# Rotating 96 images by 90 degrees: all slabs turned in pairs, every row 16 KB, the first pair stored between the loads

## The chip, the cores and the metric

The kernel runs on one core of a Trainium2 chip. The metric is device time in microseconds (us) of that core. Beside the three timed runs there is one profiled execution; its span goes from its first to its last instruction. A DMA (a transfer between HBM, the chip's main memory, and SBUF, the core's working memory of 128 partitions) is issued by an instruction on a queue, here the queue of SyncE (SP), and is carried out by 16 DMA engines as packets. VectorE is DVE in the profile, ScalarE is ACT.

## The reference

```python
x = np.random.randn(32, 3, 256, 256).astype(np.float32)
out = np.rot90(x, k=-1, axes=(-2, -1))       # out[b, c, i, j] = x[b, c, 255 - j, i]
```

Nothing is calculated: 96 images of 256 x 256 float32 values (256 KB each, 25.17 MB in all) are read, each is rotated clockwise, and 25.17 MB are written.

## The kernel before, in words

**Slabs.** The 24,576 image rows are cut into 12 slabs of 2 MB (8 images). A slab fills one tile of 128 partitions by 4096 floats, its *unit* (`units`, lines 71 to 79), and all twelve units together hold the whole input at once, 192 KB in each partition. A partition holds either 8 image rows in one piece twice over ("short" rows of 8 KB, line 63), or 16 image rows in one piece ("long" rows of 16 KB, line 66). A long slab is moved by two DMAs of 1 MB, each to every second partition (`i::I`).

**The turn.** VectorE's transpose turns 32x32 blocks: it moves data within groups of 32 partitions. Rotating a whole image therefore needs a change of layout between load and store, which the access patterns of `turn` (lines 102 to 118) make: read with the image rows spread one way, write with both orders reversed. A slab that is turned by itself has short rows on one side and long rows on the other. Slabs 0, 1 and 2 (`long_st`) are loaded short and stored long; slabs 3 to 7 are loaded long and stored short. Slabs 8 to 11 (`paired`) are turned two at a time, (8, 9) and (10, 11): one turn over both units, in four instructions, with long rows on both sides. Each instruction of a turn handles 128 x 2048 floats, so there are 24 in all.

**Homes.** A turn doesn't write where it reads. `home` (line 100) puts slab n's result into slab n-1's unit, which is free once slab n-1 has been turned. (For the pairs, the results go one pair back: lines 110 and 111.) Slab 0 has nothing before it: its result goes into `turned0`, a tile in PSUM, the other on-chip memory, which a DMA doesn't read here. At the end ScalarE copies it into the last unit by two copies (line 146), and it is stored from there (line 148).

**Queues.** All DMAs are issued by SP, in program order: the loads of slabs 0, 1, 2, 3, 7, 4, 5, 6, 8 to 11 (line 86; the first half of the last slab in two pieces, rows of 14 KB and 2 KB, line 94), then the stores of 4, 3, 5, 6, 7, 1, 2 (line 136), then those of the pairs, then slab 0's. Lines 139 and 140 hold the first store back until the 14 KB piece has landed. The DMAs share eight completion semaphores in turn: DMA number k is issued only when DMA number k-8 has landed. VectorE turns slab after slab in order of number.

Of the kernel before, what the change touches and what calls it, by code (L numbers as in the profile page):

```python
# [1 line left out]

# [4 lines left out]

@with_exitstack
def kernel(
    ctx: ExitStack,
    tc: tile.TileContext,
    x: bass.AP,
    out: bass.AP,
):

    nc = tc.nc
    fp32 = mybir.dt.float32

    B, C, H, W = x.shape
    P = nc.NUM_PARTITIONS
    RL, RS = 16, 8  # L50
    I = 2
    Q = P * RS // H
    n_slabs = B * C // (Q * I)
    last = n_slabs - 1
    F = RS * W
    long_st = (0, 1, 2)
    both = (8, 10)
    paired = [n + a for n in both for a in range(2)]

    rows_in = x.rearrange("b c h w -> (b c h) w")  # L60
    rows_out = out.rearrange("b c h w -> (b c h) w")

    def short(rows):
        return rows.rearrange("(n i p r) w -> n p i (r w)", i=I, p=P, r=RS)

    def long(rows):
        return rows.rearrange("(n i m r) w -> n i m (r w)", i=I, m=P // I, r=RL)

    ld_short, ld_long, st_short, st_long = short(rows_in), long(rows_in), short(rows_out), long(rows_out)

    units = [None] * n_slabs
    adjacent = [(3, 7), (8, 9), (10, 11)]
    pairs = []
    for us in adjacent + [(u,) for u in range(n_slabs) if all(u not in us for us in adjacent)]:
        pool = ctx.enter_context(tc.tile_pool(name=f"unit{us[0]}", bufs=1))
        held = pool.tile([P, len(us), I * F], fp32, name=f"u{us[0]}")
        for j, u in enumerate(us):
            units[u] = held[:, j]
        pairs.append(held)
    psum = ctx.enter_context(tc.tile_pool(name="psum", bufs=1, space=bass.MemoryType.PSUM))  # L80
    turned0 = psum.tile([P, I * F], fp32, name="turned0")

    def fours(t):
        return t.rearrange("p (i f) -> p i f", i=I)

    for n in (0, 1, 2, 3, 7, 4, 5, 6, *range(8, n_slabs)):
        if n in (1, 2):
            nc.sync.dma_start(out=fours(units[n]), in_=ld_short[n])
            continue
        for i in range(I):  # L90
            if n in long_st:
                ld = nc.sync.dma_start(out=fours(units[n])[:, i], in_=ld_short[n][:, i])  # L92
            else:
                cuts = (0, 14 * W, RL * W) if (n, i) == (last, 0) else (0, RL * W)
                for f0, f1 in zip(cuts, cuts[1:]):
                    ld = nc.sync.dma_start(out=units[n][i::I, f0:f1], in_=ld_long[n, i][:, f0:f1])
                    if f1 == 14 * W:
                        mark = ld

    home = [turned0] + units[:last]  # L100

    def turn(n):
        if n in long_st:
            src = fours(units[n]).rearrange("p i (r g c) -> p c r g i", r=RS, c=RL)
            dst = home[n].rearrange("p (c k r) -> p c r k", c=RL, r=RS)[:, :, ::-1, ::-1]
            parts, step = 2, RL // 2
        elif n in paired:
            if n not in both:
                return
            src = pairs[both.index(n) + 1].rearrange("p a (r g c) -> p c r g a", r=RL, c=RL)  # L110
            dst = pairs[both.index(n)].rearrange("p i (c k r) -> p c r k i", c=RL, r=RL)[:, :, ::-1, ::-1, :]
            parts, step = 4, RL // 4
        else:
            src = units[n].rearrange("p (r g c) -> p c r g", r=RL, c=RS)
            dst = fours(home[n]).rearrange("p i (c k r) -> p c r k i", c=RS, r=RL)[:, :, ::-1, ::-1, :]
            parts, step = 2, RS // 2
        for h in range(parts):
            nc.vector.transpose(out=dst[:, h * step : (h + 1) * step], in_=src[:, h * step : (h + 1) * step])  # L118

    def store(n):  # L120
        if n in paired:
            first = n if n in both else n - 1
            if n == first:
                nc.sync.dma_start(out=st_long[n].transpose([1, 0, 2]), in_=pairs[both.index(n)][::I])
                return
            for i in range(I):
                nc.sync.dma_start(out=st_long[n, i], in_=pairs[both.index(first)][n - first :: I, i])
        elif n in long_st:
            for i in range(I):
                nc.sync.dma_start(out=st_long[n, i], in_=home[n][i::I])  # L130
        else:
            return nc.sync.dma_start(out=st_short[n], in_=fours(home[n]))

    for n in range(both[0]):
        turn(n)
    for n in (4, 3, 5, 6, 7, 1, 2):
        st = store(n)
        if n == 4:
            tc.add_manual_dep(st.ins, mark.ins.name, mybir.DependencyInfo(
                mybir.DependencyClass.Sync, mybir.DependencyReason.SCHED_ONLY), reason="stores after loads")  # L140
    for n in range(both[0], n_slabs):
        turn(n)
        store(n)

    for i in range(I):
        nc.scalar.copy(out=fours(units[last])[:, i], in_=fours(turned0)[:, i])  # L146
    home[0] = units[last]
    store(0)


# [1 line left out]
_INS = ['x']  # L152
_OUTS = [((32, 3, 256, 256), 'float32')]


# [23 lines left out]
```

## Time and profile before

| what | value |
|---|---|
| three timed runs | median 123.25 us (123.1, 123.25, 123.28) |
| profiled execution, span | 121.4 us |
| what lies around the span, by the median | 123.25 - 121.4 = 1.85 us |
| first DMA issued, first transpose, end of last transpose | 0.73, 8.25, 99.06 us |
| ScalarE: table load, two copies | 1.3 us at 62.3; 3.6 us from 99.1 |
| DMAs: loads, stores | 23 and 17 |
| HBM read, written | 25.17 MB, 25.17 MB |
| granted TensorE clock | 1.000 (TensorE does nothing) |

The profile gives no total for the profiled execution apart from its span; the median of the runs stands 1.85 us above it. The 17 stores are 7 of 2 MB and 10 of 1 MB. All DMAs go through one queue, so the 16 engines work through them in the order of issue. A "packet" in the profile is one contiguous row, and each DMA ends with 16 packets of 4 bytes, one for each engine, which count up its semaphore: 40 x 16 = 640 of them.

### The profile page before, as it was taken

The page shows a single profiled execution, that of the slowest core. Times are in us where ns is not written, and L with a number is a line of the kernel's source. Part 1 is how long each engine was busy: PE and PEld are TensorE (multiplying, and loading weights), DVE is VectorE, ACT ScalarE, POOL GpSimd, SP SyncE. Part 2 cuts the span into 40 slices and gives each one's busy share as a digit, 9 for nine tenths or more (in the row PEclk, how much of TensorE's full clock was granted, in tenths as well). Part 3 has the DMA queues.
Part 4 walks back from the last instruction along what each step waited for, and adds up shares of the span by engine and source line. Part 5 has one row for each costly group of instructions (what it writes and reads, how often), then busy time and mean ns, then how long its engine had stood idle before and what let it go on. Part 6 is the DMA issues. An engine that isn't in the chain of part 4 may idle for free.

```text
span 121.4 us, 134 instructions
## 1 busy us (share of the span) xinstructions
DVE 90.5 (75%) x24; ACT 4.9 (4%) x3; POOL 0.2 (0%) x4
## 2 busy tenths in 40 slices
DVE  0029999999999999999999999999999960000000
ACT  0000000000000000000040000000000038000000
POOL 0000000000000000000000000000000000000000
DMA  3999999999999999999999999999999999999994
GB/s 84 416 432 424 426 459 432 432 432 426 426 432 426 416 421 432 421 426 450 403 424 426 426 429 429 421 432 424 464 426 432 432 432 432 432 432 432 432 432 178
DMA packets 4800, 50.33 MB, mean 414 GB/s; under 512 B 640, under 2 KB 640, under 8 KB 704
## 3 DMA queue, kind: packets, MB, share of 16 engines
q1 hardware_dynamic: 4800, 50.33, 98.0%
HBM read 25.17 MB, written 25.17 MB: 414 GB/s over the span
## 4 chain that ended last, share of the span: by engine, by line
DVE 55%; issue 17%; DMA 6%; DVEq 3%; ACT 2%; ACTq 1%; SPq 0%
DVE u L118 50%; DVE turned L118 6%; DMA u<-in_x_dram 6%; DVEq L174 3%; ACT u L146 2%; ACTq L174 1%; SPq L92 0%; DVEq L118 0%
## 5 line engine op out<-in xcount | busy, mean ns | idle before, releaser
L118 DVE STREAM_TRANSPOSE u<-u 128x2048 f32<-128x2048 f32 x22 | 83.4, 3861 | 0.3
L118 DVE STREAM_TRANSPOSE turned<-u 128x2048 f32<-128x2048 f32 x2 | 7.1, 3584 | 8.3 <-DMA u<-in_x_dram 8.3
L146 ACT COPY u<-turned 128x2048 f32<-128x2048 f32 x2 | 3.6, 1869 | 35.6 <-DVE u L118 35.6
L146 ACT ACT_TABLE_LOAD x1 | 1.3, 1283 | 62.3 <-DMA u<-in_x_dram 62.3
L163 POOL MEMSET const-uint8-127<- 128x1 uint8 x1 | 0.1, 103 | 0.0
L163 POOL MEMSET const-bfloat16-1.0<- 128x1 bf16 x1 | 0.1, 101 | 0.0
L163 POOL MEMSET const-float32-0.0<- 128x1 f32 x1 | 0.1, 99 | 0.2 <-issue 0.2
L163 POOL MEMSET const-float32-1.0<- 128x1 f32 x1 | 0.1, 99 | 0.0
## 6 DMA issues: line engine op xcount, KB each, us to landing
u<-in_x_dram SPq DMA_DIRECT2D x19, 1024.0 KB, 19.6
out_dram<-u SPq DMA_DIRECT2D x7, 2048.0 KB, 16.3
out_dram<-u SPq DMA_DIRECT2D x10, 1024.0 KB, 18.3
u<-in_x_dram SPq DMA_DIRECT2D x2, 2048.0 KB, 13.7
u<-in_x_dram SPq DMA_DIRECT2D x1, 896.0 KB, 19.3
u<-in_x_dram SPq DMA_DIRECT2D x1, 128.0 KB, 17.2
```

Source lines behind the costliest of these rows:

```text
L118: nc.vector.transpose(out=dst[:, h * step : (h + 1) * step], in_=src[:, h * step : (h + 1) * step])
L146: nc.scalar.copy(out=fours(units[last])[:, i], in_=fours(turned0)[:, i])
L163: nc = _bacc.Bacc("TRN2", target_bir_lowering=False, num_devices=1)
L174: with _tile.TileContext(nc) as tc:
```

## The change

Slabs are replaced by six *pairs* of 4 MB (16 images). Pair n fills one unit of 128 partitions by 2 x 4096 floats; six units again hold the whole input. Every pair is turned as slabs 8 to 11 were: four transposes of 128 x 2048, long rows of 16 KB on both sides. A pair is loaded by four DMAs of 1 MB (64 rows of 16 KB to every second partition, of one half of the unit) and stored by two of 2 MB (128 rows of 16 KB, from every second partition).

The result of pair n goes into the unit of pair n-1, and that of pair 0 into the unit of pair 5, which is still empty: the pairs 0 to 3 are loaded, pair 0 is turned and stored, and then the pairs 4 and 5 are loaded, the latter into the unit that pair 0 is stored from. Stores of the pairs 1 to 5 follow. `move` chains all DMAs so that they are issued in this order; the edge orders them on the queue and waits for nothing. The PSUM tile, the ScalarE copies, the short rows, the 14 KB and 2 KB pieces and the hold of lines 139 and 140 are gone. There are 24 loads and 12 stores.

```diff
-    RL, RS = 16, 8
-    I = 2
...
-    long_st = (0, 1, 2)
-    both = (8, 10)
-    paired = [n + a for n in both for a in range(2)]
+    R, I, A = 16, 2, 2
+    M = P // I
+    n_pairs = B * C // (A * I * P * R // (I * H))
+    last = n_pairs - 1
...
+    def rows(t):
+        return t.rearrange("b c h w -> (b c h) w").rearrange("(n a i m r) w -> n a m i (r w)", a=A, i=I, m=M, r=R)
...
-    psum = ctx.enter_context(tc.tile_pool(name="psum", bufs=1, space=bass.MemoryType.PSUM))
-    turned0 = psum.tile([P, I * F], fp32, name="turned0")
+        units.append(pool.tile([P, A, R * W], fp32, name=f"u{n}"))
+    queued = []
+
+    def move(out, in_):
+        dma = nc.sync.dma_start(out=out, in_=in_)
+        if queued:
+            tc.add_manual_dep(dma.ins, queued[-1].ins.name, mybir.DependencyInfo(
+                mybir.DependencyClass.NoSync, mybir.DependencyReason.SCHED_ONLY), reason="order of the queue")
+        queued.append(dma)
...
+    def load(n):
+        for a in range(A):
+            for i in range(I):
+                move(out=units[n][i::I, a], in_=x_rows[n, a, :, i])
 
     def turn(n):
...
+        src = units[n].rearrange("p a (r g c) -> p c r g a", r=R, c=R)
+        dst = units[n - 1].rearrange("p i (c k r) -> p c r k i", c=R, r=R)[:, :, ::-1, ::-1, :]
+        parts = 4
+        step = R // parts
         for h in range(parts):
             nc.vector.transpose(out=dst[:, h * step : (h + 1) * step], in_=src[:, h * step : (h + 1) * step])
 
     def store(n):
+        for a in range(A):
+            move(out=out_rows[n, a], in_=units[n - 1][a::A])
...
-    for n in (4, 3, 5, 6, 7, 1, 2):
-        st = store(n)
-        if n == 4:
-            tc.add_manual_dep(st.ins, mark.ins.name, mybir.DependencyInfo(
-                mybir.DependencyClass.Sync, mybir.DependencyReason.SCHED_ONLY), reason="stores after loads")
-    for n in range(both[0], n_slabs):
+    early = 4
+    for n in range(early):
+        load(n)
+    turn(0)
+    store(0)
+    for n in range(early, n_pairs):
+        load(n)
+    for n in range(1, n_pairs):
         turn(n)
         store(n)
-
-    for i in range(I):
-        nc.scalar.copy(out=fours(units[last])[:, i], in_=fours(turned0)[:, i])
-    home[0] = units[last]
-    store(0)
```

More of the change, by code (lines that the diff above doesn't have):

```diff
@@ L49 @@
     P = nc.NUM_PARTITIONS
-    RL, RS = 16, 8
-    I = 2
[L52 to L55, printed above, removed]
-    long_st = (0, 1, 2)
-    both = (8, 10)
-    paired = [n + a for n in both for a in range(2)]
[L60 to L79, printed above, removed]
@@ L80 @@
-    psum = ctx.enter_context(tc.tile_pool(name="psum", bufs=1, space=bass.MemoryType.PSUM))
-    turned0 = psum.tile([P, I * F], fp32, name="turned0")
[L83 to L89, printed above, removed]
-        for i in range(I):
[L91 to L98, printed above, removed]
@@ L100 @@
-    home = [turned0] + units[:last]
-    def turn(n):
[L103 to L116, printed above, removed]
+    R, I, A = 16, 2, 2
@@ new lines @@
+    M = P // I
[3 more added lines that the diff above has]
+        return t.rearrange("b c h w -> (b c h) w").rearrange("(n a i m r) w -> n a m i (r w)", a=A, i=I, m=M, r=R)
+    x_rows, out_rows = rows(x), rows(out)
+    units = []
+    for n in range(n_pairs):
+        pool = ctx.enter_context(tc.tile_pool(name=f"unit{n}", bufs=1))
+        units.append(pool.tile([P, A, R * W], fp32, name=f"u{n}"))
[6 more added lines that the diff above has]
+        queued.append(dma)
@@ L120, in store @@
     def store(n):
[L121 to L135, printed above, removed]
-    for n in (4, 3, 5, 6, 7, 1, 2):
-        st = store(n)
-        if n == 4:
-            tc.add_manual_dep(st.ins, mark.ins.name, mybir.DependencyInfo(
-                mybir.DependencyClass.Sync, mybir.DependencyReason.SCHED_ONLY), reason="stores after loads")
-    for n in range(both[0], n_slabs):
+        for a in range(A):
[8 more added lines that the diff above has]
+    for n in range(1, n_pairs):
         turn(n)
         store(n)
-    for i in range(I):
-        nc.scalar.copy(out=fours(units[last])[:, i], in_=fours(turned0)[:, i])
-    home[0] = units[last]
-    store(0)
 _INS = ['x']
```

## The prediction

> **What bounds the kernel now.** I read the page's busy times first, then its slices, then the DMA queue:
>
> ```profile
> span 121.4 us, 134 instructions
> DVE 90.5 (75%) x24; ACT 4.9 (4%) x3; POOL 0.2 (0%) x4
> ...
> DVE  0029999999999999999999999999999960000000
> ...
> DMA  3999999999999999999999999999999999999994
> ...
> q1 hardware_dynamic: 4800, 50.33, 98.0%
> ```
>
> VectorE works from slice 3 to slice 33 and is idle for the last fifth. The DMA engines are full in every slice but the first and last: packets fill 98.0% of 16 engines' span. So the 50.33 MB bound the kernel, and the chain of work that the page prints (mostly VectorE, ending at 102.7 us with the copy) doesn't set the end. What VectorE and SP do matters only if the engines run out of rows. The views of VectorE's instructions (timeline; tile u in windows 15.3:31, 31:70.1 and 70.5:99.2) and SP's waits give the sizes for that:
>
> ```profile
> 8.25 7.08 DVE L118 STREAM_TRANSPOSE turned<-u 128x2048 f32<-128x2048 f32 x2 [8.25 <-DMA u<-in_x_dram]
> 15.36 83.70 DVE L118 STREAM_TRANSPOSE u<-u 128x2048 f32<-128x2048 f32 x22
> ```
> ```profile
> L118 DVE STREAM_TRANSPOSE u<-u x4: 3971/3992/4011, 15.4 to 27.1; 128x2048 f32<-128x2048 f32 x4
> ```
> ```profile
> L118 DVE STREAM_TRANSPOSE u<-u x8: 3661/3686/3711, 70.2 to 95.4; 128x2048 f32<-128x2048 f32 x8
> ```
> ```profile
> SPq L96 <- DMA u<-in_x_dram: 32.5, 14, 4.5
> SPq L124 <- DVE u L118: 19.3, 2, 10.9
> ```
>
> The numbers are min/median/max in ns. The eight transposes of the paired form take 3.69 us, the slowest form 4.01. SP waited 14 times for an older load: only eight DMAs are in flight, and the queue still never ran dry.
>
> **The sum, by packets.** The window rates (428 GB/s in 18.5:54, 428 in 63:83, 431 in 89:117) count whole packets at window edges and can't resolve a part in 500. The trace's packet records can; mean duration by size and stage:
>
> ```
> row      stage (us)      packets   ns each
> 8 KB     loads, 6-17         570   309.5 (median 309)
> 16 KB    loads, 21-50        763   613.9
> 8 KB     stores, 64-82       938   309.0
> 16 KB    stores, 88-116      736   611.0
> 14 KB    load piece           64   538.6
> 2 KB     load piece           64    84.4
> 4 B      semaphore           640     9
> ```
>
> On one engine the next packet's record starts some 3 ns before the last one's ends, so each costs 3 ns less. Each of the 16 engines gets 1/16 of the packets:
>
> - Before: 48 short loads x 306 + 68 long loads x 611 + 4 x (535.6 + 81.4) + 80 short stores x 306 + 56 long stores x 608 + 40 semaphores x 6 = 14,688 + 41,548 + 2,468 + 24,480 + 34,048 + 240 = 117,472 ns.
> - After: 96 x 611 + 96 x 608 + 36 x 6 = 58,656 + 58,368 + 216 = 117,240 ns.
>
> The working holds before: the first packet starts at 1.77 us and takes 1.31 instead of 0.31 (1.0 of first access), so the last should end at 1.77 + 1.0 + 117.5 = 120.2; the records' last ends at 120.28. **The change saves 232 ns**: 1 ns per 16 KB where loads were short, 4 ns where stores were, 24 ns each for the cut row and four semaphores. That is 0.19%, just what a measurement of this kernel can tell from no change (0.2%, or 0.25 us).
>
> The Trainium skill has a rule against this: "DMA: Bandwidth & Descriptors", Rules for kernel authors, advises one transfer over 128 partitions instead of two over disjoint halves; in the change every DMA touches only every second partition. The rows above disagree: such DMAs move 16 KB in 614 or 611 ns, those over 128 partitions in 618. By the rule the change would lose, by the rows it gains 0.2%.
>
> **Does anything run dry?** Engine time from 2.75 us (1.77 + 1.0), 9.8 us per loaded pair (16 x 611 + 24) and 9.74 per stored one. Pair 0 is through at 12.55; records of landing come 0.35 later (120.62 against 120.28), so VectorE starts at 13.0 instead of 8.25. A paired turn took 14.42 us (70.22 to 84.64).
>
> ```
> queue order   L0-L3 end   S0     L4     L5     S1     S2     S3     S4     S5
> engines done  41.95       51.7   61.5   71.3   81.0   90.8   100.5  110.2  120.0
> turn done     -           27.4   -      -      41.8   56.3   70.7   85.1   99.5
> engines need  -           41.95  -      -      71.3   81.0   90.8   100.5  110.2
> ```
>
> The smallest cover is 10.7 us, at S5; 1.04 of it is the time from issue to first packet (0.73 to 1.77). If paired turns beside loads cost the slowest row, 4.01 us a part, the last one ends at 109.3 and S5 starts about 0.1 late. So VectorE's 4.75 us later start and its faster form are worth nothing.
>
> The change adds one wait: L5 goes into the unit that S0 is stored from, so SP holds L5's first DMA until S0 has landed, 47.2 for its first half, 52.05 if both are asked for. Behind it on SP stand the rest of L5 and all later stores. The engines have L4 until 61.5, and 61.5 - 52.05 - 1.04 leaves 8.4 us. S0 waits for turn 0 (27.4) in front of L4's issue; L0 to L3 last until 41.95. The eight-semaphore limit: L4 may be issued when L2's DMAs land (25 to 32), S1 when L4's do (54); all behind work that lasts longer. An L96 load issues in 0.47 us, a store of S0's form (L124) in 0.64; 36 issues are about 19 us of a 100 us window.
>
> Taken away at nothing: ScalarE's copies (3.6 us, then SP's last two stores, issued from 102.8 on, while stores queued before them landed until 115.8) and its table load, beside other work at 62.3. The hold of the first store to 59.4 lay under loads that landed until 62.2.
>
> **What before doesn't show.** (1) The step from stores back to loads, at 51.7 us. Its nearest rows: load to store cost nothing visible (the first store landed 4.91 us after the last load, where later ones of its kind stood 4.87 apart: 0.04), and the first load of all paid 1.0 us for its first access. Bounds: 0 to 1.0 us; a gain is excluded since the engines are already full there. I take 0, because the nearer row is the one inside a full queue, where reads run ahead of the writes. The Trainium skill ("DMA: Bandwidth & Descriptors", Latency and other measured facts) gives HBM access as 0.2 us on average but 2 us under high load; uncovered, that would make the sum about 125.0. (2) The start with 16 KB rows. Ten engines started by 1.86 us, six at 2.46 to 2.66, and the first DMA's semaphores came at 4.88 to 5.24. Half as many rows per DMA may even this out; the issue is 0.06 longer (0.47 against 0.41). Bounds: -0.3 to +0.3, I take 0. (3) Which engine ends last: ends lay between 119.83 and 120.28, so luck moves the end by 0.2 either way.
>
> **Forecast**: span 121.4 - 0.23 = 121.2, plus the 1.85 around it: **123.0 us**.
>
> **Rivals.**
> - *The turn from stores to loads is exposed.* For: every engine has to fetch from HBM again after 9.7 us of SBUF reads, and the start shows 1.0 us for that. Against: load to store was free, and L4 is queued 20 us ahead. Time 123.0 + up to 1.0 = 124.0; slower by over 0.2% once more than 0.48 us is exposed. Chance 0.20: 0.14 slower, 0.06 within 0.2%.
> - *VectorE's last turn is late.* For: 14.42 us was seen only beside stores. Against: no row is over 4.01, which costs 0.1. At 4.3 us a part turn 5 ends at 13.0 + 103.2 = 116.2, and S5 starts 7 us late: 130. It decides from 4.0 on. Chance 0.06, slower.
> - *Short rows cost more than their packets' median.* Loads of slabs 1 and 2 landed at 8.15 to 18.09: 2.49 us per MB, against 2.45 for long ones (20.54 to 57.24 for 15 MB). Were all of that due to the form, 6 MB x 0.04 more goes: 122.75. Against: part of it is the start, which stays. Chance 0.08, faster.
> - *It does nothing*: the 232 ns are eaten by reads' stalls (long loads range from 611 to 620 ns, and there are more of them): 123.25. Chance 0.04, the same.
> - The forecast itself: 0.62, of which 0.38 under 123.0 (faster by over 0.2%) and 0.24 above it.
>
> Faster 0.38 + 0.08 = 0.46; same 0.24 + 0.06 + 0.04 = 0.34; slower 0.14 + 0.06 = 0.20. The range: 122.6 (the third rival with half of the start's gain) to 124.0 (the first rival in full); the late turn and some luck are left out. The forecast's own range is 122.8 to 123.2.
>
> **What would show it.** Right: 3648 packets (3072 rows, 576 of 4 B); DMA slices at 9 from the second to the last but one; transposes from about 13 to 100 us; SP waiting for S0 before L5 but no dip of the rate near 61; a span of 121.2. Wrong: a slice at 52 us with a smaller DMA share or lower GB/s (first rival); transposes above 4.0 us and a dip at 110 (second); a dip at 61, which would mean that L5 is held longer than S0's landing.

## The result, and the profile after

| | before | after |
|---|---|---|
| median of 4 runs each | 123.2 us (123.1 to 123.28) | 124.69 us (124.51 to 125.12) |
| ratio, 95% interval | | 1.0127 (1.0109 to 1.0146) |
| span of the profiled execution | 121.4 us | 122.9 us |

The change costs 1.3%, about 1.5 us. The forecast was 123.0, and its range ended at 124.0. From the page of the kernel after, the lines that answer to those of before, with the rate of each slice:

```profile
span 122.9 us, 125 instructions
...
DVE 86.3 (70%) x24; POOL 0.2 (0%) x4
...
DVE  0000599999999999999999999999999950000000
...
DMA  2999999999999999999999999999999999999992
GB/s 64 416 427 443 427 432 432 427 432 427 427 427 427 299 427 427 437 432 432 432 432 437 443 421 427 437 427 427 432 427 432 427 432 427 427 443 437 427 437 96
...
q1 hardware_dynamic: 3648, 50.33, 96.6%
```

The packets are the 3648 foreseen, and the engines are full from the second slice to the last but one, as they were. Yet they are busy for 96.6% of the span instead of 98.0%, and one slice moves 299 GB/s where its neighbours move 427. It is the fourteenth, 40 to 43 us: the step from the loads of pair 3 to the store of pair 0. The *busy* share doesn't show the loss, since a packet that is kept waiting counts as busy; the *rate* does. That is the first thing to read here. The windows of the kernel after (length, VectorE's and POOL's busy time, clock, DMA share, GB/s) narrow it down:

```profile
39.00:42.00 3.00, 3.00 (x1) 0.00 (x0) 1.00 1.02 344
42.00:45.00 3.00, 2.97 (x2) 0.00 (x0) 1.00 0.89 371
54.00:57.00 3.00, 2.97 (x2) 0.00 (x0) 1.00 1.02 431
```

At 39 to 42 the share is 1.02 and the rate 344: rows that last longer. VectorE and the SP queue did what was foreseen. VectorE's timeline, its instructions on tile u, and SP's waits, after:

```profile
13.53 86.49 DVE L58 STREAM_TRANSPOSE u<-u 128x2048 f32<-128x2048 f32 x24 [13.53 <-DMA u<-in_x_dram]
```
```profile
L58 DVE STREAM_TRANSPOSE u<-u x24: 3662/3684/3722, 13.5 to 96.3; 128x2048 f32<-128x2048 f32 x24
```
```profile
SPq L41 <- DVE u L58: 33.3, 5, 12.8
SPq L41 <- DMA u<-in_x_dram: 32.8, 19, 2.0
...
SPq L41 <- DMA out_dram<-u: 12.7, 2, 8.3
```

All 24 transposes lie between 3662 and 3722 ns, beside loads and beside stores alike, and the last ends at 100.0. The stores of pair 5 are issued right then, 12 us before the engines get to them. SP's two waits for a store (12.7 us in all) are L5's, and nothing runs dry behind them.

**Where 1.48 us come from.** The records of landing (when a DMA's last engine has counted up its semaphore), one profiled execution against the other (121.43 and 122.91 us; Ln and Sn are the loads and the stores of pair n, and a "step" is the time from one DMA's landing to the next one's):

```
                                          before     after     difference
first 2 MB landed                           8.15      8.51       +0.36
first change, L3 -> S0:  last load's step      -      3.41       +0.96   (undisturbed 2.45)
second change, S0 -> L4: last two stores'      -   4.90, 4.97     +0.34   (undisturbed 4.86,
                  and first two loads' steps       then 2.62, 2.48           then 2.45)
third change, L5 -> S1                         -      4.92       +0.06   (undisturbed 4.86)
all other transfers                          112.47   112.04      -0.43   (by difference)
last landing to end of span                   0.81      1.00      +0.19
sum                                                               +1.48
```

The 112.47 runs from 8.15 to the last landing at 120.62. After, it is 8.51 to 121.91, 113.40, less the 1.36 of the three changes. So in this execution the rows did bring a gain, and it was given back four times over. The packet records of one engine show what the largest item looks like (start : ns of each row, the last load's four and the first of the store):

```
39.62:612  40.23:922  41.14:1293  42.43:853 | 43.29:611 ...
```

Three rows of 16 KB take 0.92, 1.29 and 0.85 us instead of 0.61. All 16 engines show it between 40.1 and 43.3, about half of them losing some 0.5 us and half some 1.2 (mean 0.91). It is the *load's* rows that are slow, those ahead of the change; the store's are at full speed from its first row.

### The profile page after: what moved, and what is told of

The parts are those of the page before. It is cut to its first block, busy times and chain, and to the rows that moved or that the text cites. A ratio compares the mean times of both kernels' runs of the same rounds, so it can differ in the third digit from the quotient of the medians.

```text
span 122.9 us, 125 instructions
## 1 busy us (share of the span) xinstructions
DVE 86.3 (70%) x24; POOL 0.2 (0%) x4
## 2 busy tenths in 40 slices
DMA packets 3648, 50.33 MB, mean 410 GB/s; under 512 B 576, under 2 KB 576, under 8 KB 576
## 3 DMA queue, kind: packets, MB, share of 16 engines
q1 hardware_dynamic: 3648, 50.33, 96.6%
## 4 chain that ended last, share of the span: by engine, by line
DMA 48%; DVE 25%; DVEq 3%; SPq 2%; issue 2%
DMA u<-in_x_dram 48%; DVE u L58 25%; DVEq L99 3%; SPq L41 2%; DVEq L58 0%
## 5 line engine op out<-in xcount | busy, mean ns | idle before, releaser
L58 DVE STREAM_TRANSPOSE u<-u 128x2048 f32<-128x2048 f32 x24 | 86.3, 3687 | 13.7 <-DMA u<-in_x_dram 13.5
```

## The experiments

Each kernel is the one after with one edit, unless "before" or more edits are said. Medians stand with the ratio to the kernel before, timed beside each (123.18 to 123.26), and its 95% interval. A "change of direction" is a place in the queue where a store follows a load or a load a store. "Delay" is the extra time there, mean of 16 engines by packet records. "Spread" is the time between the first and the last of the 16 engines to finish the last DMA that is not delayed yet; where it is small, the engines are called "in step". One execution of each kernel was profiled, and runs of one kernel differ by up to 1.7 us (e1: 124.39 to 126.06), so each delay is a single sample.

### Is it the queueing ahead, or the place between the loads?

In before, the hold of lines 139 and 140 let the first store be issued only when the loads were nearly through; after, S0 is issued at 27.9 us, some 15 us before the engines get to it. Theory A: this costs the 0.96. Rival B: a store between loads costs it, whenever issued.

**e1_hold**, after `store(0)`:

```diff
+    tc.add_manual_dep(queued[16].ins, queued[14].ins.name, ...Sync...)   # S0 until the 15th load landed
```

> The changed kernel, with pair 0's store held on SP until the 15th load has landed (40.3 us), as the kernel before held its first store; nothing else differs. In the changed kernel the last load before that store landed 3.41 us after the one ahead of it instead of 2.45: a stall of 0.96 us on all 16 engines. Theory A (stores that stand in the queue long before the loads ahead of them end slow those loads' last rows): the stall goes, landing step 2.5, span 122.9 - 0.9 = 122.0, time about 123.8. Theory B (a store with loads behind it stalls, whenever it is issued): nothing changes, 122.9 and 124.7. Theory C (the first store of the program pays for its first access): nothing changes either.

Measured: **125.43**, 1.0172 (1.012 to 1.0224), span 124.3. The windows of e1, with the columns as above:

```profile
39.00:42.00 3.00, 3.00 (x1) 0.00 (x0) 1.00 0.94 399
42.00:45.00 3.00, 2.96 (x2) 0.00 (x0) 1.00 1.01 431
51.00:54.00 3.00, 3.00 (x2) 0.00 (x0) 1.00 1.11 350
54.00:57.00 3.00, 2.96 (x2) 0.00 (x0) 1.00 0.95 404
69.00:72.00 3.00, 2.96 (x2) 0.00 (x0) 1.00 1.01 333
```

The stall at 40 us is gone (last load's step 2.46, S0's 4.86). But there are two new ones, at 51 to 56 us (S0's second half 5.41 instead of 4.86, L4's first load 3.32 instead of 2.45) and at 69 to 72 (3.62). By packets they cost 0.94 and 0.80; in the kernel after, the same two changes cost 0.04 and 0.03. A holds for the change that is held, and fails for the kernel: the loss moves on. C falls, since the program's first store now costs nothing; B's forecast of no change fails at the first change, too.

**e2_no_store_between**: S0 goes to the end of the queue.

```diff
-    store(0)
     for n in range(early, n_pairs):
...
+    store(0)
```

> The changed kernel with pair 0's store moved to the end of the queue, behind all other stores, so that loads and stores don't alternate; the bytes, rows and DMAs are the same. It leaves out the right values of pair 0: its result is overwritten by pair 5's load, and pair 5's unturned rows are stored in its place. The first store, pair 1's, now stands some 17 us ahead of the end of the loads. Theory A: the stall of 0.96 us appears at the end of the last load, span 122.7, time 124.5. Theory B: no stall anywhere, span 122.9 - 1.2 = 121.7, time 123.5. Theory C: a stall of about 1 us at the first store, as A.

Measured: **124.21**, 1.0079 (1.0062 to 1.0096), span 122.4. With a single change from loads to stores the stall is still there, at 60 to 63 us (322 GB/s, delay 0.68). So B isn't needed for it; the two other changes are worth about 0.5 us.

**e3_before_no_hold**: before without lines 138 to 140.

> The kernel before without the hold of its first store (lines 138 to 140): that store is issued some 12 us earlier, at 47.5, as soon as its semaphore is free. Theory A: the last loads' rows are slowed by about 1 us, span 121.4 + 1.0 = 122.4, time 124.2. Theories B and C: no change (121.4, 123.2).

Measured: **123.44**, 1.002 (1.0011 to 1.003). The hold is worth 0.2 us in before. Before and e3, the same window (VectorE, ScalarE, POOL, clock, share, GB/s):

```profile
60.00:63.00 3.00, 2.97 (x2) 0.74 (x1) 0.00 (x0) 1.00 0.97 412
```
```profile
60.00:63.00 3.00, 2.96 (x2) 0.79 (x1) 0.00 (x0) 1.00 0.96 393
```

Without its hold before loses only 0.11 (mean), a fraction of what the pairs lose. "Queued ahead" alone isn't the cause.

**e4_early3**: `early = 3` instead of 4, so S0 comes after three pairs.

> The changed kernel with three pairs loaded ahead of pair 0's store instead of four; that store is issued when its turn ends (27.9 us), only some 4.5 us before the loads ahead of it end (32.5) instead of 14.5. Theory A: the stall shrinks with the time that the store stands in the queue, to under 0.4 us, span about 122.3, time 124.1. Theories B and C: the stall of 1 us moves to 30 to 33 us, span 122.9, time 124.7.

Measured: **124.92**, 1.0142 (1.012 to 1.0165). The stall moves with the change (the twelfth load's step is 3.42, delay 0.98), and it doesn't shrink to the 0.4 that A foresaw. It belongs to the change of direction, not to a moment or to VectorE's second turn.

### The engines in step

In e1 the engines came to the second change within 0.29 us of each other, in the kernel after 0.89 apart: its first stall had split them into two groups of eight, 0.76 apart. Theory D: a change is dear when the 16 engines get to it together, and nearly free when they get to it one group after the other. Rival E: the form of the store decides (before stored short rows first).

**e5_hold_all**: S0's second half in two DMAs, and holds at all three changes.

```diff
+    hold(queued[16], queued[14])
+    hold(queued[19], queued[17])
+    hold(queued[27], queued[25])
```

> The changed kernel with all three changes of direction issued just in time: pair 0's store held until the 15th load has landed, pair 4's load until the first half of the last 2 MB of that store has landed (it is stored as two DMAs of 1 MB for that), pair 1's store until the 24th load but one has landed. Holding the first alone took that stall away (15th to 16th landing 2.46 us instead of 3.41) and two others of 1.4 and 1.2 us came up at the next two changes. Theory A (what stands in the queue long before a change of direction slows the rows in front of it): all three are gone, span 122.9 - 1.3 = 121.6, time 123.4. Theory D (engines that run in step collide at a change of direction, and a stall spreads them, which spares the next change): one or more of the stalls stay, span 122.5 or more, time above 124.2.

Measured: **125.31**, 1.0169 (1.0148 to 1.019). First change 0, third 0.26, but the second (stores to loads) 1.29, so A fails here and D's forecast holds. A load issued just ahead of the change costs no less than one queued early, and keeping the engines in step through the first change leaves them in step for the second.

**e6_skew**: a load of 8 rows of 15 KB more, which half of the engines carry, after pair 0's loads, to push the engines apart.

```diff
+        if n == 0:
+            move(out=spare, in_=x_rows[0, 0, 0:8, 0, :3840])
```

> The changed kernel with one more small load behind pair 0's: 8 rows of 15 KB into a spare tile, which only 8 of the 16 engines carry, so that these run some 0.57 us behind the others from then on. It adds 0.12 MB that nobody uses. Theory D: at the first change of direction the mean delay of the engines falls from 0.9 us to under 0.3; the 8 engines end 0.57 later than without, so span about 122.6, time 124.4. Theory A: the delay of 0.9 us stays and comes on top: span 123.3, time 125.1.

Measured: **125.53**, 1.0192 (1.0175 to 1.0208). Windows of e6:

```profile
12.00:15.00 3.00, 0.77 (x1) 0.00 (x0) 1.00 1.14 243
39.00:42.00 3.00, 3.00 (x2) 0.00 (x0) 1.00 1.00 426
42.00:45.00 3.00, 2.96 (x2) 0.00 (x0) 1.00 1.03 437
```

426 and 437 where after has 344 and 371: no stall at any of the three changes (longest row 0.66 us). The kernel is slower all the same, since the small DMA itself held up all engines at 12.7 us: by 1.7 us those that don't carry it, by 2.2 to 2.6 those that do, their own row included. D's forecast of the delay held, not that of the time. The offset wasn't tried alone, since that stall came first.

**e7_store_short**: S0 with 8 KB rows over all 128 partitions.

```diff
+    for a in range(A):
+        move(out=short_rows[a], in_=units[last][:, a].rearrange("p (i f) -> p i f", i=2))
```

> The changed kernel with pair 0's store alone moved in another form: 8 KB rows from all 128 partitions, as the kernel before stored slabs 3 to 7, instead of 16 KB rows from every second partition. The values of pair 0 land in wrong places; bytes and DMAs are the same. In the kernel before without its hold, the same change of direction into 8 KB stores cost 0.11 us on average. Theory E (the form of the store decides: half of the partitions): the delay of 0.9 us at the first change falls under 0.3, span 122.9 - 0.7 + 0.1 = 122.3, time 124.1. Theories A and D: it stays, 123.0 and 124.8.

Measured: **124.66**, 1.0113 (1.009 to 1.0136). The stall stays (step 3.32, delay 0.81, spread 0.45). E falls.

### The start and the end

**e8_start_split**: the very first load in two column pieces, rows of 8 KB to the same 64 partitions.

```diff
+                cuts = (0, R * W // 2, R * W) if (n, a, i) == (0, 0, 0) else (0, R * W)
```

> The changed kernel with its very first load of 1 MB cut into two of 0.5 MB with 8 KB rows. In the changed kernel the first issue took 0.60 us against 0.41 before, the first packet started at 2.22 against 1.77, and the first 2 MB landed at 8.51 against 8.15. If the 16 KB row is what makes the first issue slow, the first packet starts at 1.8 and 2 MB have landed by 8.2; span 122.6, time 124.4. If not, 8.5, and 122.9 to 123.0, 124.7.

Measured: **125.21**, 1.0163 (1.0122 to 1.0204). The first DMA's issue still takes 0.603 us (before 0.407, after 0.597) and the first packet still starts at 2.11 (1.77, 2.13 and not 2.22). The length of the rows isn't what makes the start late.

**e9_close**: all the terms found so far undone together. The first two loads are short over 128 partitions, S0 comes between S4 and S5, the stores of pairs 3 and 4 are split in two, and the first store is held.

> The sum closed: the changed kernel without the four things that the runs so far have put beside the forecast. Pair 0's store goes between the stores of the pairs 4 and 5 instead of between the loads; the first store is held until the 23rd load has landed; the very first two loads are 8 KB rows over 128 partitions, as before; the stores of the pairs 3 and 4 are four DMAs of 1 MB each, so that there are 40 DMAs as before. It leaves out the right values of pair 0 (its result is overwritten, pair 5's unturned rows are stored in its place, and 8 images are loaded into other partitions). If the packets' sum was right and the loss lies in these four, span 121.4 - 0.2 = 121.2, time 123.0. If the sum was wrong too (16 KB rows from every second partition cost more than their records say), 121.7 or more, time above 123.5.

**e10_start_tail**: of these, the start and the split stores alone.

```diff
+                if n == a == 0:
+                    move(out=units[0][:, 0].rearrange("p (i f) -> p i f", i=I)[:, i], in_=short_in[0][:, i])
...
+            if n in (3, 4):
+                for i in range(I):
+                    move(out=out_rows[n, a][:, i], in_=units[n - 1][a::A, i])
```

> The changed kernel with two of the four alone: the very first two loads as 8 KB rows over 128 partitions (8 images land in other places) and 40 DMAs instead of 36 (the stores of the pairs 3 and 4 in four pieces). Cutting the first load's rows had not moved the first packet (2.11 us) or the first issue (0.60 us), so the form with 64 rows of every second partition is suspected instead. If that is it, the first packet starts at 1.8 us and 2 MB have landed by 8.15 instead of 8.31 to 8.51. The span ends 0.8 us after the last landing instead of 1.0, since the last DMA then uses the semaphore that SP asks for last. Span 122.9 - 0.3 - 0.2 = 122.4, time 124.2, give or take the stalls; if neither matters, 124.7.

Measured: e9 **123.2**, 1.0002 (0.9993 to 1.0011), span 121.4; e10 **124.07**, 1.0081 (1.0054 to 1.0109), span 122.1. The start and the end of before are back in both: first packet at 1.73 and 1.81, 2 MB landed at 8.11 and 8.15, the last landing 0.81 ahead of the end. The first windows of after and e10:

```profile
0.00:3.00 3.00, 0.00 (x0) 0.20 (x4) 1.00 0.23 66
```
```profile
0.00:3.00 3.00, 0.00 (x0) 0.20 (x4) 1.00 0.37 76
```

The end depends on the number of DMAs. When the last has landed, SP asks the semaphores of the final DMAs one after the other, some 0.07 us each. With 36 DMAs the last one uses a semaphore after which SP asks three times more; with 40, as in before, it uses the one that is asked last, and 0.19 us go. From the last packet to the end of the span it is 1.15 to 1.16 us in the five kernels with 40 DMAs (before, e3, e9, e10, e14), 1.21 in the one with 39 (e11), and 1.32 to 1.36 in all with 36 or 37. In e10 the stall at 40 us is left alone and still there (step 3.33).

e9 accounts for the loss: with these terms undone, it is gone. It also says where the *gain* of the rows went: there the long stores take 614 to 617 ns a row instead of 611. All stores take 58.60 us; at the 4.85 us from landing to landing that one of 2 MB takes late in the kernel after, they would take 58.2. That is about what the other rows save. (e9 is no version to use: S0's values are gone by then.)

### Four rivals of "in step"

e3 left a question: before without its hold loses 0.1, the pairs 0.7 to 1.1. What is different? F: the piece of 2 KB that before has at its change. G: the number of DMAs queued behind the change. H: VectorE's work beside it.

**e11_before_no_hold_no_cut**: e3, the last slab's first half in one piece.

```diff
-                cuts = (0, 14 * W, RL * W) if (n, i) == (last, 0) else (0, RL * W)
+                cuts = (0, RL * W)
```

> The kernel before without the hold of its first store, and with the last slab's first half loaded in one piece (16 KB rows instead of 14 KB and 2 KB). Without the hold alone, the engines were delayed by 0.11 us on average at the change from loads to stores, though they ran in step (spread 0.25 us); the changed kernel lost 0.9 there. Theory F (the short rows shortly ahead of the change protect it): 0.7 us or more now, span 122.1 or more, time above 123.9. Theory G (the kernel before is spared for another reason, such as fewer DMAs in the queue): 0.1 again, span 121.6, time 123.4.

**e12_cut**: after, with pair 3's last half cut as in before.

> The changed kernel with the last load but one ahead of pair 0's store cut into rows of 14 KB and 2 KB, as the kernel before has it, and no hold. Theory F: the delay at the first change of direction falls from 0.9 us to 0.1 to 0.3. A spared first change leaves the engines in step, so the next one may then cost up to 0.9 (theory D); time 123.9 to 124.8. Theory G: the delay of 0.9 stays.

Measured: e11 **123.67**, 1.0038 (1.0025 to 1.0052), delay 0.27; e12 **124.67**, 1.0121 (1.0094 to 1.0148), the stall unchanged (step 3.43, delay 1.0). F falls; the cut is worth some 0.2 in before.

**e13_hold_loads_only**: L4 is held until S0's first half has landed, so only two DMAs stand behind the change.

```diff
+    tc.add_manual_dep(queued[18].ins, queued[16].ins.name, ...Sync...)
```

> The changed kernel with the loads behind pair 0's store held on SP until the first half of that store has landed; the store itself isn't held. At the first change of direction only two DMAs (the store's) then stand behind the loads instead of six. Theory G (the number of DMAs queued behind the change makes the stall): the mean delay at the first change falls from 0.9 us to 0.3 or less, time 124.1 or less if the next change costs no more than before. Theory D (engines in step, whatever stands behind the store): 0.8 to 1.0 us there as before, and little at the next two changes, time 124.5 to 124.9.

**e14_before_long_first**: e3 with the stores in the order 1 to 7, long rows first.

> The kernel before without its hold and with the stores in the order 1, 2, 3, 4, 5, 6, 7, so that seven DMAs stand behind the last load instead of three, the first of them with 16 KB rows from every second partition. With its own order and no hold it lost 0.11 us on average at that change. Theory G: 0.6 us or more, span 122.0 or more, time above 123.8. If the order and number of stores don't matter: 0.1 to 0.3, time 123.4 to 123.6.

Measured: e13 **124.66**, 1.012 (1.0079 to 1.016), delay 0.92 with two DMAs queued. e14 **130.27**, 1.0566 (1.0546 to 1.0587): in this order VectorE had to wait 12.0 us for a unit that was still being stored, so its time says nothing of the question; but at its change seven DMAs were queued and the delay was 0.23. G falls on both sides.

**e15_no_turns**: the turns of pairs 1 to 5 left out, their units stored as they are.

```diff
     for n in range(1, n_pairs):
-        turn(n)
         store(n)
```

> The changed kernel with the turns of the pairs 1 to 5 left out: each pair is loaded, and the rows of the unit before it are stored unturned, so that the values of these pairs are wrong. Pair 0 is turned as before, and the order of all DMAs and what holds them on SP around the first two changes of direction is the same; VectorE is idle from 28 us on. Theory H (VectorE's paired transposes beside the DMAs make the stall at the first change, and the kernel before runs another form there): no delay at 41 us, span about 121.9, time 123.7. Theory D alone (engines in step): the delay of 0.8 to 1.0 us at 41 us is still there, little at the next changes, span 122.5 to 123.0, time 124.3 to 124.8.

Measured: **124.52**, 1.0104 (1.0087 to 1.0121). Windows of e15, VectorE's busy time in the second column:

```profile
39.00:42.00 3.00, 0.00 (x0) 0.00 (x0) 1.00 1.00 306
42.00:45.00 3.00, 0.00 (x0) 0.00 (x0) 1.00 0.88 360
```

VectorE does nothing and the rate still falls to 306 (delay 1.08). H falls: the stall doesn't need the turns beside it.

**e16_skew_first**: e6's small load as the first DMA of all, where nothing is queued yet that it could hold up.

```diff
+    move(out=spare, in_=x_rows[0, 0, 0:8, 0, :3840])
     for n in range(early):
```

> The changed kernel with one more small load as the very first DMA: 8 rows of 15 KB into a spare tile, which only 8 of the 16 engines carry; 0.12 MB that nobody uses. Behind pair 0's loads the same small load had itself stalled all engines for some 1.1 to 2.5 us at 12.7 us, and none of the three changes of direction stalled after that; so it wasn't the offset alone that was tried. At the head of the queue nothing is in flight that it could stall. Theory D (engines in step collide at a change of direction): the two halves stay about 0.57 us apart up to 41 us, and the mean delay at the first change is under 0.3 us instead of 0.9; span 122.9 - 0.7 + 0.3 = 122.5, time 124.3. If the offset doesn't matter, or an earlier stall is what spares the later changes: 0.8 to 1.0 us at the first change, span 123.3, time 125.1.

Measured: **124.93**, 1.0115 (1.0072 to 1.0158). The start is 1.2 later, which is the small load's doing. At the first change, at 43 to 46 us here, only four engines of 16 stall, by about 1 us each: the delay is 0.24, where after has 0.91. So D's forecast of the delay (under 0.3) holds, and that of the time is missed by the late start. Windows of e16, with a dip to 404 instead of 344:

```profile
39.00:42.00 3.00, 3.00 (x2) 0.00 (x0) 1.00 1.05 437
42.00:45.00 3.00, 2.97 (x2) 0.00 (x0) 1.00 1.00 404
```

### All changes of direction together

```
                                        spread (us)         delay (us)
pairs, loads -> stores, not held    after .44, e2 .54, e4 .50, e7 .45, e10 .23,
  engines in step                     e12 .62, e13 .52, e15 .35           .68 to 1.08
                                    e8 (14 of 16 within .36)              .84
                                    e1, third change (12 of 16 in .25)    .80
stores -> loads, in step            e1 .29; e5, held                      .94; 1.29
loads -> stores, held               before, e1, e5, e9; e5's third        0; .26
stores -> loads, apart              after .89, e4 .77, e7 .70, e10 .96, e12 .78,
                                      e13 1.19, e15 .95, e16 1.52         0 to .17
loads -> stores, apart              after 1.24, e4 1.54, e7 .70, e10 1.11,
                                      e12 1.33, e13 1.21, e15 .95, e16 1.49   0 to .12
halves pushed apart                 e6, three changes; e16's first .49    0; .24
e8's second and third change        14 of 16 within .38 at both           0; .01
before's slabs, not held            e3 .25, e11 .68, e14 .36              .11 to .27
```

In the pair kernels every loss of 0.68 us or more fell on a change that at least 12 of the 16 engines reached within 0.35 us of each other. Where no 12 were that close, a change cost 0.26 us at most. That border rests on few changes: with 12 engines within 0.345 us e12 lost 1.0, with 12 within 0.36 us e16 lost 0.24.

The reverse doesn't hold. In e8, 14 of 16 engines came to the second and third change as close together as to its first, and lost nothing. The windows of e8 at the three changes:

```profile
39.00:42.00 3.00, 3.00 (x2) 0.00 (x0) 1.00 1.04 344
51.00:54.00 3.00, 3.00 (x1) 0.00 (x0) 1.00 1.01 431
69.00:72.00 3.00, 3.00 (x1) 0.00 (x0) 1.00 1.01 431
```

Nor is it simply that an earlier stall spares the later changes: e1 lost 0.80 at its third after 0.94 at its second. Before's slabs don't fit either: in e3 and e14 they change in step and lose 0.1 to 0.2. **This is open.** Every large loss goes with engines in step, and e6 and e16, which set the spread from outside, make it likely that this is needed, in one profiled execution each. That it is *enough* is refuted by e8, e3 and e14. What the engines collide on isn't shown. No run varies by itself which places in HBM and SBUF the DMAs at a change touch, so that rival is untested.

The slow rows are those ahead of the change, and holding the store back removes them (e1), so the DMAs behind the change seem to be at work already. The Trainium skill ("DMA: Bandwidth & Descriptors", Two DMAs through the same engine are not ordered) says that an engine's reads and writes are separate queues, and that descriptors start in order but overlap; this fits that a store's reads slow the writes of the load ahead of it, but no run here shows the two sides apart.

## Why the prediction was wrong, step by step

- **The bound**: right. The engines are full, and VectorE and SP don't set the end.
- **The sum by packets, -0.23**: the direction was right, and in the profile the transfers outside the changes took 0.43 less. But in e9, with everything else undone, the gain came to nothing, because long stores cost 614 to 617 ns and not 611. The duration of a row had been taken as a property of its form, and that isn't all of it. What else decides isn't shown; the spread alone doesn't: the long stores took 611 in before (spread about 0.45) and in e2 (0.78), and 615 to 622 in e5 (0.77).
- **The cover** (VectorE's later start, the last turn, L5's wait for S0): right. A part took 3.66 to 3.72 us beside loads as beside stores, so the rival of a late last turn falls.
- **"Load to store cost nothing visible (0.04)"** and **"the hold of the first store ... lay under loads"**, taken away at nothing: this is the step that failed. The forecast had no cost for the change from L3 to S0, and it cost 0.96 of the 1.48 us. The row was read rightly, but it was that of a change which the hold had *protected*: the trace showed the price of a held change, and the change forecast had none. The hold was counted as a wait that hides under other work, when it also kept stores out of the queue while loads ran. e1 shows that a hold takes the stall away here, and that then the next changes pay. The missing hold is only part of the answer, though: e3 prices it in before at 0.2 us (delay 0.11), so even a row without a hold would have foretold far too little. Why the same change costs the pairs 0.68 to 1.08 stays open.
- **Stores back to loads, 0 out of 0 to 1.0**: by landings 0.34. The mean engine loses only 0.04, but the engines had just been split, and a DMA has landed when its last engine has. In e1 and e5, in step, it costs 0.94 and 1.29, near and beyond the upper bound. That it cost little here is luck: nothing in the working speaks of how the engines stand to each other, and the first stall had split them. The slice at 52 us that was to betray this rival shows nothing; the dip is at 40, where none was looked for.
- **The start, 0 out of -0.3 to +0.3**: +0.36, just outside. In the nine other kernels whose first two loads are the same, 2 MB had landed at 8.31 to 8.48, 0.16 to 0.33 after before's 8.15, so part of it is the one execution. Issue is 0.19 longer (0.597 against 0.407), and the first packet is 0.36 later. The working put the issue at 0.06 more, by rows from the middle of the queue. The Trainium skill's rule on disjoint halves ("DMA: Bandwidth & Descriptors", Rules for kernel authors), weighed and set aside in the prediction, would have paid at this one place: e10's start over 128 partitions gets the 0.36 back. In the full queue the halves cost nothing: 611 ns a row against 2 x 309.
- **The end**: not priced at all, and +0.19. Four DMAs fewer were counted as 24 ns saved.
- **The range**: its upper end took the worst of one unknown term, 1.0, and none of the others. All its upper bounds together, with the start's 0.3 and luck's 0.2, make 124.5, still below 124.69, because two terms weren't in the sum at all: the first change and the end.

## What to carry to other kernels

A row of the trace prices an operation only under the conditions that it was measured in: if the change also removes a wait near it, ask what that wait kept apart before taking it away at nothing. In a kernel bound by a full DMA queue, read the rate and the rows' durations around each change of direction, not the engines' busy share, and count two changes of direction more as two prices more. When the expected gain is 0.2%, the first issue and the last semaphore are as large as the gain, and each belongs in the sum.

## What the runs showed of the hardware

- A change from loads to stores in a full queue can slow the last two or three 16 KB rows ahead of it on all 16 engines, from 0.61 to between 0.7 and 1.3 us (after; delay 0.68 to 1.08 in nine pair kernels). With the store held until the loads are nearly through it cost nothing in before, e1, e5 and e9, and 0.26 us at e5's third change. A change from stores to loads cost 0.94 us in e1 and, though held, 1.29 in e5; in the ten others that have one it cost 0 to 0.17.
- A load of only 8 rows in a full queue held up all 16 engines by 1.7 us or more (e6).
- The first DMA's issue takes 0.58 to 0.60 us to every second partition and 0.37 to 0.41 to all 128; its first packet starts at 2.1 or at 1.73 to 1.81 us.
- From the last landing to the end of the span it is 0.81 or 1.00 us (before, after), by which semaphore the last DMA uses.
